# A decoder layer on one core: folded weight chunks begun before a group of seven, turns one step later, and a twelfth group with sums made ahead

## The chip, the core and the metric

The kernel runs on one core of a Trainium2 chip. The metric is device time of one execution in microseconds (us); the kernel before takes 2227.09 us, the median of 3 runs. A matmul here has a weight tile of 128x128 and streams 512 columns. TensorE is PE, VectorE DVE, ScalarE ACT, GpSimd POOL, and SyncE, which issues most transfers, SP.

## What is computed

A decoder layer for 256 tokens of width 2048 in float32: half a SwiGLU feed-forward, then retention and windowed attention side by side, a second half feed-forward, and a gated embedding, each with a layer norm behind it. The change touches the two feed-forwards:

```python
def swiglu(x, w_gu, w_down):
    g, u = jnp.split(x @ w_gu, 2, axis=-1)
    return (jax.nn.silu(g) * u) @ w_down
...
    h = layer_norm(alpha * h + 0.5 * swiglu(h, w_ffn1_gu[i], w_ffn1_down[i]), ln_g[i, 0], ln_b[i, 0])
...
    h = layer_norm(alpha * h + 0.5 * swiglu(h, w_ffn2_gu[i], w_ffn2_down[i]), ln_g[i, 2], ln_b[i, 2])
```

`w_gu` is 2048 x 11264, `w_down` 5632 x 2048.

## The kernel before

Every float32 factor is split in two parts, high and low, and a product is three matmuls: high by low, high by high, low by high (L431 to L433). The tokens' parts stay on chip, the weights stream through. A **chunk** is 512 KB of weights. SP loads it raw (L119), ACT casts it to the high part (L105), DVE subtracts the high part from the raw chunk for the low part (L106), PE uses both.

The work is a list of units (`plan`), each of them a pair of chunks or one chunk, written in the order in which PE will use them:

- **Single**: one chunk, 12 matmuls, one cast, one subtract. "P" is two Singles.
- **Folded**: one chunk whose low part DVE does not make. ACT multiplies the raw chunk by −1 into the place of the low part (here with the high part ahead of it in the order of `make`), POOL issues a transfer that adds the raw chunk to it (L170), and ACT casts the high part. "F" is a Single and a Folded, 24 matmuls.
- **Seven** ("S"): a pair of chunks as a product with seven instead of eight sub-products, 21 matmuls rather than 24, at the price of four sums (L226 to L229) and four subtracts on DVE and four casts on ACT.
- **Prepared** ("D"): a Seven whose sums were made earlier, in the mixer stages, by `sums_ahead` (L298 to L311), stored to DRAM, and are loaded back: one subtract for each of two raw tiles, four more loads.

A feed-forward's first product goes through 11 columns (j) of 512, each with 8 pairs p of chunks in the depth. Column 0 is eight P. Feed-forward 1 orders the others "FFSSFSSP": pairs 4 and 5 folded, Sevens 0 and 1, pair 6 folded, Sevens 2 and 3, pair 7. In feed-forward 2, `AHEAD` (L44) lists the columns with Prepared groups: odd columns 1 to 7 have two, even columns 2 to 6 one ("P?SSDSSP"), eleven in all; column 8 is "PFSSFSSP", 9 and 10 are as in feed-forward 1. The second product has four blocks of 512 output columns, done two at a time, so that a pair of chunks p (22 of them) serves two blocks; `FIRST_DOWN` (L51) orders the pairs of the first such block.

What sets the order ahead of PE is `fill` (L316). It runs each time that PE is done with a unit. It makes loaded units (casts, sums, subtracts) while less than 45 matmuls are ready, and loads further units of the plan while less than 90 are ready or loaded, as long as slots are free. All tiles live in a pool of 46 slots (`SLOTS`); `slots_for_weights` says how many the planner may use in a stage: 24 in feed-forward 1, 36 − j in feed-forward 2. A Folded's multiplication and transfer so begin in the place that the chunk has in the plan.

When a column is done, its result is activated and **turned** (`turned`, L984): cast into two 16-bit words on ACT, transposed by a transfer that SP issues (L189), joined on ACT. `later(DELAY, ...)` puts the transpose one step (one unit) after the words and the joining three steps behind it. The turned data is the left factor of the second product.

At the end of a block with Sevens, `seven_common` (from L546) combines four partial sums on ACT and DVE (`eve`, `evw`), which frees the banks that the next block writes.

Of the kernel before, what the change touches and what calls it, by code (L numbers as in the profile page):

```python
# [9 lines left out]
F32R = mybir.dt.float32r  # L10
# [40 lines left out]
FIRST_DOWN = "PPPPPPFFSFSPSFSPSFSSPS"  # L51
SECOND_DOWN = "PPPSPSPSFSPSFSSPSPPPPP"
LEAD = 4

# [8 lines left out]
def layer(ctx: ExitStack, tc: tile.TileContext, io):  # L63
# [24 lines left out]
    plan = []  # L88
# [51 lines left out]
    class Single:  # L140
# [7 lines left out]
        def load(self, **how):  # L148
            self.chunk = Chunk(self.key, **how)
# [1 line left out]
        def make(self):  # L151
            self.chunk.make()

    class Folded:

        loads, makes, keeps, time = 1, 2, 2, 12

        def __init__(self, key):  # L160
            self.key = key

        def load(self, **how):
            self.chunk = Chunk(self.key, **how)

        def make(self):
            c = self.chunk
            c.make_hi()
            act.mul(c.lo, c.raw, -1.0)
            pool.dma_start(c.lo, c.raw, accum_op=ALU.add)  # L170
            act.copy(c.hi, c.raw)

    class Turn:

# [141 lines left out]
    def fill(must=False):  # L316

        while True:
            queued = sum(u.time for u in ready)
            left = room["slots"] - room["used"]  # L320
            wanted = must and not ready or not room["quiet"] and queued < room["ahead"]
            if loaded and wanted and loaded[0].makes <= left:
                u = loaded.pop(0)
                u.make()
                room["used"] += u.keeps - u.loads
                ready.append(u)
                continue
            first = loaded[0] if loaded else plan[0] if plan else None
            queued += sum(u.time for u in loaded)
            if plan and queued < room["far"] and plan[0].loads + first.makes <= left:  # L330
                u = plan.pop(0)
                u.load()
                room["used"] += u.loads
                loaded.append(u)
                continue
            return

    def make_next():
# [4 lines left out]
        ready.append(u)  # L343

    def take(key):
        if not ready:
            fill(True)
        u = ready.pop(0)
        assert u.key == key, (u.key, key)
        return u  # L350
# [5 lines left out]
    def slots_for_weights(n, ahead=45, far=90):  # L356
        room.update(slots=n, ahead=ahead, far=far)
# [616 lines left out]
    def ffn(name, i, ht, norm, keep, residual, keepers, away):  # L974
# [33 lines left out]
        for j in range(KF // 4):  # L1008
            pg, pu = banks(f"{name}g{j}"), banks(f"{name}u{j}")
            units = gu_units(name, j)  # L1010
            n_of = {(0, 0): KD, (0, 1): KD, (1, 0): KD, (1, 1): KD}
            for kind, p in units:
                if kind in "SD":
                    for at in ((0, 0), (0, 1), (1, 0)):
                        n_of[at] -= 1
                    n_of[1, 1] -= 2
            sums = [[Sum((pg, pu)[n][t], n_of[t, n]) for n in range(2)] for t in range(2)]
            got = []

            if norm is not None and j == 0:  # L1020
                front, units = units[:FRONT_PAIRS], units[FRONT_PAIRS:]
                steps = [(gu_keys(name, 0)(n, p), 2 * p, n) for _, p in front for n in range(2)]
                norm.by_transfer = 3,
                norm.first(steps, rhs, sums, (
                    (3, (1, 0)), (5, "more"), (5, (1, 1)), (7, (0, 2)), (8, (1, 2)), (9, (0, 3)), (9, (1, 3)),
                    (10, ("move", 3)), (10, "go"),
                ))
                later(1, lambda: norm.join(3))
                slots_for_weights(24)

            def before(u, j=j, offset=KD // 2 - len(units)):
                u += offset
                if j == 0 and norm is None and u % 2 == 0:
                    first_chunk(u // 2)
                    if u == 6:
                        slots_for_weights(24)
                    if u == 2:
                        load_constants()
                if j == 0 and u == 7:
                    for g in sorted({p // 2 for p in SEVEN}):  # L1040
                        hi, lo = (slot([P, 8, P], F32R, f"{name}f{w}{g}") for w in "hl")
                        made[g] = seven_forms(keep[g], hi, lo)
                    if name == "f2":
                        g = AHEAD[1][0] // 2
                        made[g] = forms_of([ht[:, 4 * g : 4 * g + 4, :]], f"{name}f{g}")
                if name == "f2" and j and u == 0:
                    slots_for_weights(AHEAD_SLOTS - j)
                if j == KF // 4 - 1 and u in (4, 6):
                    convert(u // 2 - 2)

            block(f"{name}{j}", units, gu_keys(name, j), rhs, forms, sums, lambda *a: got.extend(seven_common(*a)), before)
            if got:
                g, v = got
                for x, ps in ((g, pg), (v, pu)):
                    for t in range(2):
# [158 lines left out]
    def mixers(ht, norm, residual, keepers, away):  # L1214
# [295 lines left out]

        made = {}
        forms = lambda p: made[p // 2](p % 2)
        lazy.append(sums_ahead(ahead[6:9], 2, 2))
        slots_for_weights(18)
        sig = []
        for j in range(4):
# [76 lines left out]

        lhs = lambda k: of_pairs(mix_t, k)
        slots_for_weights(16)
        lazy.append(sums_ahead(ahead[9:], 3, 2))

        def residual_added(blk, ps):
            for t in range(2):
# [344 lines left out]
```

## Time and profile before

| | us |
|---|---|
| median of 3 runs | 2227.09 (2226.49 to 2227.42) |
| the profiled execution | 2230.62 |
| its span in the profile | 2228.6 |
| PE busy in it | 2218.5 |
| DVE busy | 2004.0 |
| ACT busy | 1439.0 |
| POOL busy | 50.9 |

The span of the profile reaches from the first to the last instruction; the execution's own time is 2.0 us longer. Busy times are sums over the whole span. A row of a wait gives the waiting engine and line, what it waited for, and then the sum, the number and the longest of these waits. A row of a window gives the stretch, its length, busy time of each engine with its number of instructions, the granted clock of PE as a share, the busy share of the DMA engines, and GB/s.

### The profile page before, as it was taken

Reading aid. Unit: us, or ns where it says so; the run is one execution under the profiler, and the core shown is the slowest. Engines: PE = TensorE matmul, PEld = TensorE weight load, DVE = VectorE, ACT = ScalarE, POOL = GpSimd, SP = SyncE. Lnnn points to the kernel's source line nnn. Section 1 sums busy time; section 2 is a strip of 40 time slices with the busy share of each in tenths; the row PEclk is TensorE's granted clock in tenths of the full one; section 3 lists DMA queues with packets and bytes.
Section 4 is the critical chain, followed back from the end, with each engine's and each line's share of the span. In section 5 each row is a group of like instructions: output and inputs, shape, how many; then the busy total and the mean of one; then the engine's idle time right before and its main releaser. Section 6 shows DMA issues by size and latency. Waiting matters only on the chain.

```text
span 2228.6 us, 29103 instructions
## 1 busy us (share of the span) xinstructions
PE 2218.5 (100%) x10140; PEld 1838.9 (83%) x10140; DVE 2004.0 (90%) x2624; ACT 1439.0 (65%) x1677; POOL 50.9 (2%) x65
## 2 busy tenths in 40 slices
PE   9999999999999999999999999999999999999998
PEld 8888888888888888888788888888888888888887
DVE  6999999989998789789999888779999999999977
ACT  6777777777565545557865567466766677765653
POOL 0000000000000000000000000000000000000000
PEclk9999999999999999999999999999999999999999
DMA  9988998976686889757976568888999999666871
GB/s 321 250 264 252 249 263 241 269 227 217 228 305 234 298 283 338 203 179 232 291 233 226 184 203 321 316 302 266 301 301 295 300 248 276 209 233 221 309 283 68
DMA packets 302075, 570.51 MB, mean 256 GB/s; under 512 B 98652, under 2 KB 103388, under 8 KB 301928
## 3 DMA queue, kind: packets, MB, share of 16 engines
q1 hardware_dynamic: 291880, 536.71, 72.3%
q0 software_dynamic: 8064, 29.36, 7.0%
q10 hardware_dynamic: 1984, 2.58, 0.4%
q8 instruction: 79, 1.29, 0.2%
q14 instruction: 68, 0.56, 0.1%
HBM read 487.32 MB, written 31.46 MB: 233 GB/s over the span
## 4 chain that ended last, share of the span: by engine, by line
PE 93%; DMA 3%; DVE 2%; issue 1%; ACT 0%; SPq 0%; ACTq 0%; POOL 0%; DVEq 0%; POOLq 0%
PE rqk L382 3%; PE f2g L431 3%; PE f2g L433 3%; PE f2g L432 3%; PE f1g L431 2%; PE f1g L433 2%; PE f1g L432 2%; PE f2u L431 2%; PE f2u L433 2%; PE f2u L432 2%; PE f1u L433 2%; PE f1u L431 2%; PE f1u L432 2%; PE aqk L382 2%; PE f2e L431 1%; PE f1e L431 1%
## 5 line engine op out<-in xcount | busy, mean ns | idle before, releaser
L106 DVE TENSOR_TENSOR lf_gu<-rf_gu,hf_gu 128x1024 fp32r<-128x1024 f32 (+1 forms) x225 | 267.7, 1210 | 22.1 <-ACT hf_gu L105 21.1
L105 ACT CAST hf_gu<-rf_gu 128x1024 fp32r<-128x1024 f32 (+1 forms) x225 | 228.7, 1039 | 22.1 <-DMA rf_gu<-in_f_gu 21.5
L106 DVE TENSOR_TENSOR lw_in_f<-rw_in_f,hw_in_f 128x1024 fp32r<-128x1024 f32 x140 | 167.8, 1219 | 15.0 <-ACT hw_in_f L105 15.0
L106 DVE TENSOR_TENSOR lf_down<-rf_down,hf_down 128x1024 fp32r<-128x1024 f32 x130 | 155.7, 1220 | 12.9 <-ACT hf_down L105 11.1
L105 ACT CAST huf_gu<-uf_gu 128x1024 fp32r<-128x1024 f32 x76 | 80.1, 1053 | 125.4 <-DVE uf_gu L227 109.4
L105 ACT CAST hf_down<-rf_down 128x1024 fp32r<-128x1024 f32 x130 | 132.7, 1049 | 30.5 <-DMA rf_down<-in_f_down 21.3
L105 ACT CAST hw_in_f<-rw_in_f 128x1024 fp32r<-128x1024 f32 x140 | 140.4, 1049 | 2.3 <-PE gt L433 1.6
L105 ACT CAST hvf_gu<-vf_gu 128x1024 fp32r<-128x1024 f32 x76 | 80.1, 1054 | 32.4 <-DVE vf_gu L229 30.5
L106 DVE TENSOR_TENSOR luf_gu<-uf_gu,huf_gu 128x1024 fp32r<-128x1024 f32 x76 | 92.6, 1218 | 0.0
L106 DVE TENSOR_TENSOR lvf_gu<-vf_gu,hvf_gu 128x1024 fp32r<-128x1024 f32 x76 | 92.6, 1218 | 0.0
L431 PE MATMUL f1g<-hf_gu,xt 128*128 128x512 f32 x232 | 90.8, 391 | 0.0
L433 PE MATMUL f1g<-lf_gu,xt 128*128 128x512 f32 x232 | 90.5, 390 | 0.0
L432 PE MATMUL f1g<-hf_gu,xt 128*128 128x512 f32 x232 | 90.5, 390 | 0.0
L431 PE MATMUL f2g<-hf_gu,ht 128*128 128x512 f32 x211 | 82.2, 390 | 0.0
L433 PE MATMUL f2g<-lf_gu,ht 128*128 128x512 f32 x211 | 82.1, 389 | 0.0
L432 PE MATMUL f2g<-hf_gu,ht 128*128 128x512 f32 x211 | 82.1, 389 | 0.0
L433 PE MATMUL f1u<-lf_gu,xt 128*128 128x512 f32 x192 | 75.0, 391 | 1.2 <-DMA lf_gu<-rf_gu 1.2
L431 PE MATMUL f1u<-hf_gu,xt 128*128 128x512 f32 x192 | 74.7, 389 | 0.0
L432 PE MATMUL f1u<-hf_gu,xt 128*128 128x512 f32 x192 | 74.7, 389 | 0.0
L170 POOL DMA_DIRECT2D lf_gu<-rf_gu x42 | 36.4, 867 | 1641.2 <-DMA rf_gu<-in_f_gu 1017.6
L105 ACT CAST huf_down<-uf_down 128x1024 fp32r<-128x1024 f32 x32 | 33.7, 1054 | 60.7 <-DVE uf_down L227 58.7
L1057 ACT ACTIVATE eve<-eve 128x1024 f32<-128x1024 f32 x20 | 21.2, 1061 | 67.3 <-DVE eve L1056 67.3
(1512 smaller groups left out, 6978.3 us busy)
## 6 DMA issues: line engine op xcount, KB each, us to landing
rf_gu<-in_f_gu SPq DMA_DIRECT2D x361, 512.0 KB
rf_down<-in_f_down SPq DMA_DIRECT2D x176, 512.0 KB
rw_in_f<-in_w_in_f SPq DMA_DIRECT2D x148, 512.0 KB
lf_gu<-rf_gu POOLq DMA_DIRECT2D x42, 512.0 KB, 8.2
rw_rv<-in_w_rv SPq DMA_DIRECT2D x32, 512.0 KB
rw_ret<-in_w_ret SPq DMA_DIRECT2D x32, 512.0 KB
rw_mix<-in_w_mix SPq DMA_DIRECT2D x32, 512.0 KB
rw_pg<-in_w_pg SPq DMA_DIRECT2D x32, 512.0 KB
```

The lines of the kernel that those rows point to most:

```text
L105: act.copy(dst_hi, src)
L106: (lo_engine or dve).tensor_tensor(dst_lo, src, dst_hi, ALU.subtract)
L170: pool.dma_start(c.lo, c.raw, accum_op=ALU.add)
L382: pe.matmul(ps[f], hi[:, kk, f * P : (f + 1) * P], rhs(k), start=k == 0, stop=k == n_k - 1,)
L431: pe.matmul(o, al, bh, start=first, stop=False)
L432: pe.matmul(o, ah, bh, start=False, stop=False)
L433: pe.matmul(o, ah, bl, start=False, stop=self.left == 0)
L1057: act.activation(g, g, AF.Silu)
```

## The change

Folded is cut in two. A Folding, which takes no time on PE, loads the chunk, multiplies it and begins the accumulating transfer; the Folded that is left casts the high part at its old place and frees the Folding's two slots. `fold_at` puts the Folding into the plan 34 matmuls ahead of the Folded for first products and 12 for the second; if a Seven stands there or up to twelve units before, it goes back to just ahead of the nearest one. `AHEAD` gains pair 4 of column 8, so that column's order becomes "PFSSDSSP" and twelve groups have their sums made ahead, the second list of them with one group more. `DELAY` becomes 2. `FIRST_DOWN` gets one more F, and its two adjacent Sevens (17 and 18) are parted by pair 20. The first feed-forward's planner may use 30 slots.

```diff
+FOLD_AHEAD = 12, 34
-AHEAD = {1: (4, 5), 2: (4,), 3: (4, 5), 4: (4,), 5: (4, 5), 6: (4,), 7: (4, 5)}
+AHEAD = {1: (4, 5), 2: (4,), 3: (4, 5), 4: (4,), 5: (4, 5), 6: (4,), 7: (4, 5), 8: (4,)}
-DELAY = 1
+DELAY = 2
-FIRST_DOWN = "PPPPPPFFSFSPSFSPSFSSPS"
+FIRST_DOWN = "PPPPPFFSFSFSPSFSPSFSPS"
...
-    class Folded:
-        loads, makes, keeps, time = 1, 2, 2, 12
+    class Folding:
+        loads, makes, keeps, time = 1, 1, 2, 0
...
         def make(self):
             c = self.chunk
-            c.make_hi()
+            c.lo = slot(list(c.raw.shape), F32R, "l" + c.name)
             act.mul(c.lo, c.raw, -1.0)
             pool.dma_start(c.lo, c.raw, accum_op=ALU.add)
+
+    class Folded:
+        loads, makes, keeps, time = 0, 1, 2, 12
+        def __init__(self, begun):
+            self.key, self.begun = begun.key, begun
+        def load(self):
+            pass
+        def make(self):
+            c = self.chunk = self.begun.chunk
+            c.hi = slot(list(c.raw.shape), F32R, "h" + c.name)
             act.copy(c.hi, c.raw)
+            room["used"] -= self.begun.keeps
+
+    def fold_at(ahead, key):
+        begun = Folding(key)
+        at, time = len(plan), 0
+        while at > 0 and time < ahead:
+            at -= 1
+            time += plan[at].time
+        if ahead and any(isinstance(u, Seven) for u in plan[at - 12 : at + 1]):
+            while not isinstance(plan[at], Seven):
+                at -= 1
+        plan.insert(at, begun)
+        plan.append(Folded(begun))
...
             elif kind == "F":
-                plan.extend(of(keys(n, p)) for n, of in enumerate((Single, Folded)))
+                plan.append(Single(keys(0, p)))
+                fold_at(FOLD_AHEAD[keys(1, p)[0][-3:] == "_gu"], keys(1, p))
...
-                        slots_for_weights(24)
+                        slots_for_weights(30)
...
-        lazy.append(sums_ahead(ahead[3:6], 2, 2))
+        lazy.append(sums_ahead(ahead[3:7], 2, 2))
```

(The other two lists shift by one; `fill` and `take` leave units without time out of the ready list.)

ACT at the end of column 5 of feed-forward 1. In a name such as `hf1_gu_6_1_4`, h is a high part (l a low part, r raw, u and v sums), then stand the column, the chunk of the pair, and the pair; the last number counts tiles. Before:

```order
L105 CAST hvf1_gu_5_0_2_2123<-vf1_gu_5_0_2_2107 128x1024
L105 CAST hf1_gu_5_0_3_2147<-rf1_gu_5_0_3_2051 128x1024
L105 CAST bf1_gu_5_0_3_2151<-rf1_gu_5_1_3_2053 128x512
L105 CAST huf1_gu_5_0_3_2154<-uf1_gu_5_0_3_2141 128x1024
L105 CAST hvf1_gu_5_0_3_2158<-vf1_gu_5_0_3_2142 128x1024
L196 COPY f1a4_2164<-mf14_2055 128x2x4x128 x2
L105 CAST hf1_gu_5_0_7_2179<-rf1_gu_5_0_7_2083 128x1024
L105 CAST hf1_gu_5_1_7_2206<-rf1_gu_5_1_7_2127 128x1024
L105 CAST hf1_gu_6_0_4_2235<-rf1_gu_6_0_4_2162 128x1024
L169 ACTIVATE lf1_gu_6_1_4_2240<-rf1_gu_6_1_4_2183 128x1024
L171 CAST hf1_gu_6_1_4_2239<-rf1_gu_6_1_4_2183 128x1024
```

And of the change, where the multiplication is L170 and the cast L187:

```order
L107 CAST hvf1_gu_5_0_2_2127<-vf1_gu_5_0_2_2111 128x1024
L170 ACTIVATE lf1_gu_6_1_4_2145<-rf1_gu_6_1_4_2054 128x1024
L170 ACTIVATE lf1_gu_6_1_5_2148<-rf1_gu_6_1_5_2056 128x1024
L107 CAST hf1_gu_5_0_3_2157<-rf1_gu_5_0_3_2058 128x1024
L107 CAST bf1_gu_5_0_3_2161<-rf1_gu_5_1_3_2060 128x512
L107 CAST huf1_gu_5_0_3_2164<-uf1_gu_5_0_3_2151 128x1024
L107 CAST hvf1_gu_5_0_3_2168<-vf1_gu_5_0_3_2152 128x1024
L107 CAST hf1_gu_5_0_7_2186<-rf1_gu_5_0_7_2085 128x1024
L226 COPY f1a4_2190<-mf14_2087 128x2x4x128 x2
L107 CAST hf1_gu_5_1_7_2214<-rf1_gu_5_1_7_2131 128x1024
L107 CAST hf1_gu_6_0_4_2241<-rf1_gu_6_0_4_2172 128x1024
L187 CAST hf1_gu_6_1_4_2245<-rf1_gu_6_1_4_2054 128x1024
```

The multiplications of pairs 4 and 5 of column 6 went from behind pair 7 of column 5 to ahead of its fourth Seven (pair 3); the joining (COPY) moved one chunk back.

SP's loads for column 8 of feed-forward 2 (chunk 0 or 1, then the pair). Before:

```order
L119 DMA rf2_gu_8_0_6_16017<-in_f2_gu 128x2x512
L119 DMA rf2_gu_8_1_6_16031<-in_f2_gu 128x2x512
L119 DMA rf2_gu_8_0_2_16069<-in_f2_gu 128x2x512
L119 DMA rf2_gu_8_1_2_16071<-in_f2_gu 128x2x512
L119 DMA rf2_gu_8_0_3_16089<-in_f2_gu 128x2x512
L119 DMA rf2_gu_8_1_3_16091<-in_f2_gu 128x2x512
L189 DMA_TRANSPOSE mf27_16093<-wf27_16033 128x16x128
```

And of the change:

```order
L121 DMA rf2_gu_8_0_4_16044<-in_f2_gu 128x2x512
L287 DMA rf2_gu_8_0_4b_16046<-in_f2_gu 128x2x256
L291 DMA huf2_gu_8_0_4_16048<-hudf2_gu_8_0_4_12589 128x1024
L291 DMA luf2_gu_8_0_4_16050<-ludf2_gu_8_0_4_12590 128x1024
L291 DMA hvf2_gu_8_0_4_16052<-hvdf2_gu_8_0_4_12591 128x1024
L291 DMA lvf2_gu_8_0_4_16054<-lvdf2_gu_8_0_4_12592 128x1024
L121 DMA rf2_gu_8_0_2_16068<-in_f2_gu 128x2x512
L121 DMA rf2_gu_8_1_2_16070<-in_f2_gu 128x2x512
L121 DMA rf2_gu_9_1_4_16169<-in_f2_gu 128x2x512
L121 DMA rf2_gu_9_1_5_16171<-in_f2_gu 128x2x512
L121 DMA rf2_gu_8_0_3_16173<-in_f2_gu 128x2x512
L121 DMA rf2_gu_8_1_3_16175<-in_f2_gu 128x2x512
```

The Prepared group's six loads took the place of a folded pair, and two chunks of column 9 now stand ahead of the loads of the fourth Seven (pair 3).

SP's loads at the end of the first down block of feed-forward 1 (block, then the pair). Before:

```order
L119 DMA rf1_down_0_20_4717<-in_f1_down 128x1024
L119 DMA rf1_down_1_20_4777<-in_f1_down 128x1024
L119 DMA rf1_down_0_17_4779<-in_f1_down 128x1024
L119 DMA rf1_down_1_17_4781<-in_f1_down 128x1024
L119 DMA rf1_down_0_18_4803<-in_f1_down 128x1024
L119 DMA rf1_down_1_18_4805<-in_f1_down 128x1024
L119 DMA rf1_down_0_21_4911<-in_f1_down 128x1024
L119 DMA rf1_down_1_21_4938<-in_f1_down 128x1024
L119 DMA rf1_down_0_19_4965<-in_f1_down 128x1024
L119 DMA rf1_down_1_19_4967<-in_f1_down 128x1024
```

And of the change:

```order
L121 DMA rf1_down_1_20_4740<-in_f1_down 128x1024
L121 DMA rf1_down_0_17_4742<-in_f1_down 128x1024
L121 DMA rf1_down_1_17_4744<-in_f1_down 128x1024
L121 DMA rf1_down_0_20_4766<-in_f1_down 128x1024
L121 DMA rf1_down_0_18_4833<-in_f1_down 128x1024
L121 DMA rf1_down_1_18_4835<-in_f1_down 128x1024
L121 DMA rf1_down_0_21_4853<-in_f1_down 128x1024
L121 DMA rf1_down_1_21_4911<-in_f1_down 128x1024
L121 DMA rf1_down_0_19_4913<-in_f1_down 128x1024
L121 DMA rf1_down_1_19_4915<-in_f1_down 128x1024
```

Pair 20 moved between the Sevens 17 and 18, its second chunk, which is folded, ahead of 17.

More of the change, by code (lines that the diff above doesn't have):

```diff
@@ L152, in make, with load @@
             self.chunk.make()
-    class Folded:
-        loads, makes, keeps, time = 1, 2, 2, 12
+    class Folding:
+        loads, makes, keeps, time = 1, 1, 2, 0
         def __init__(self, key):
             self.key = key
-        def load(self, **how):
-            self.chunk = Chunk(self.key, **how)
+        def load(self):
+            self.chunk = Chunk(self.key)
         def make(self):
             c = self.chunk
-            c.make_hi()
+            c.lo = slot(list(c.raw.shape), F32R, "l" + c.name)
             act.mul(c.lo, c.raw, -1.0)
             pool.dma_start(c.lo, c.raw, accum_op=ALU.add)
-            act.copy(c.hi, c.raw)
+    class Folded:
+        loads, makes, keeps, time = 0, 1, 2, 12
+        def __init__(self, begun):
+            self.key, self.begun = begun.key, begun
+        def load(self):
+            pass
+        def make(self):
+            c = self.chunk = self.begun.chunk
+            c.hi = slot(list(c.raw.shape), F32R, "h" + c.name)
+            act.copy(c.hi, c.raw)
+            room["used"] -= self.begun.keeps
[10 more added lines that the diff above has]
+        plan.append(Folded(begun))
     class Turn:
@@ L322, in fill @@
             if loaded and wanted and loaded[0].makes <= left:
[L323 to L326, printed above, removed]
+                make_next()
                 continue
@@ L342, in make_next @@
         room["used"] += u.keeps - u.loads
-        ready.append(u)
+        if u.time:
+            ready.append(u)
     def take(key):
-        if not ready:
+        while not ready:
             fill(True)
@@ L1512, in mixers @@
         forms = lambda p: made[p // 2](p % 2)
-        lazy.append(sums_ahead(ahead[6:9], 2, 2))
+        lazy.append(sums_ahead(ahead[7:10], 2, 2))
         slots_for_weights(18)
@@ L1595, in mixers @@
         slots_for_weights(16)
-        lazy.append(sums_ahead(ahead[9:], 3, 2))
+        lazy.append(sums_ahead(ahead[10:], 3, 2))
         def residual_added(blk, ps):
```

## The prediction

> **What bounds the kernel now.** I read the page's busy line first, then the chain that ended last, then PE's waits, and only then the stages.
>
> ```profile
> PE 2218.5 (100%) x10140; PEld 1838.9 (83%) x10140; DVE 2004.0 (90%) x2624; ACT 1439.0 (65%) x1677; POOL 50.9 (2%) x65
> DVE  6999999989998789789999888779999999999977
> PEclk9999999999999999999999999999999999999999
> PE 93%; DMA 3%; DVE 2%; issue 1%; ACT 0%; SPq 0%; ACTq 0%; POOL 0%; DVEq 0%; POOLq 0%
> ```
>
> PE works in 2218.5 of 2228.6 us, at full granted clock throughout, and 93% of the chain is PE. DVE, at 90%, is close behind and owns 2% of the chain; DMA owns 3%. So there are two ways to save time: fewer matmuls, or the few places where PE waits. PE's list of waits names them:
>
> ```profile
> PE f1u L433 <- DMA lf_gu<-rf_gu: 1.2, 2, 0.9
> PE f1e L431 <- DVE evw L550: 0.6, 1, 0.6
> PE mr1a L433 <- DVE lw_ret L106: 0.5, 1, 0.5
> PE f2e L431 <- DVE evw L550: 0.5, 1, 0.5
> ```
>
> The change touches three of these four rows: the two waits for an accumulating transfer (first row), and the turn from the first to the second block of each down product (f1e, f2e). The third lies in the mixers, whose own order is not edited. Columns of the feed-forwards, cut at their first matmul, show what a column costs:
>
> ```profile
> core 0: us, PE busy (x) PEld busy (x) DVE busy (x) ACT busy (x) POOL busy (x), PEclk, DMA share, GB/s
> 50.10:92.10 42.00, 41.12 (x182) 33.73 (x181) 37.64 (x46) 30.53 (x34) 2.58 (x3) 1.00 0.97 270
> 92.10:132.90 40.80, 40.80 (x182) 33.78 (x181) 38.61 (x47) 29.53 (x33) 2.60 (x3) 1.00 0.82 237
> 214.50:255.90 41.40, 41.06 (x181) 33.67 (x180) 38.56 (x47) 31.54 (x35) 2.59 (x3) 1.00 0.96 251
> 378.30:419.30 41.00, 41.00 (x181) 33.71 (x180) 38.60 (x47) 30.82 (x34) 2.58 (x3) 1.00 0.92 254
> 460.10:574.40 114.30, 114.30 (x506) 94.64 (x505) 104.92 (x123) 80.55 (x85) 4.32 (x5) 1.00 0.69 222
> 874.60:900.00 25.40, 25.40 (x124) 21.45 (x123) 22.07 (x51) 11.96 (x15) 0.00 (x0) 1.00 0.80 269
> 900.00:923.20 23.20, 23.20 (x107) 19.30 (x106) 15.65 (x21) 16.08 (x21) 0.00 (x0) 1.00 0.96 285
> 1694.90:1735.10 40.20, 40.20 (x179) 33.26 (x179) 38.75 (x47) 27.34 (x31) 0.86 (x1) 1.00 0.93 304
> 1775.20:1816.00 40.80, 40.80 (x182) 33.78 (x181) 38.61 (x47) 29.49 (x33) 2.58 (x3) 1.00 0.90 258
> ```
>
> The rows are columns 1, 2, 5 and 9 of feed-forward 1, its first down block, two pieces of the retention stage, and columns 6 and 8 of feed-forward 2. A column of 180 matmuls takes 40.80 us undisturbed, that is 40.80/180 = 0.2267 us a matmul. Columns 1, 5 and 9 take 1.2, 0.6 and 0.2 us more, and in 1 and 5 the DMA share is 0.97 and 0.96.
>
> **The accumulating transfers.** A Folded chunk's low part is an ACT multiplication, then a transfer that POOL issues. The chain through column 1, and below it the one through column 5:
>
> ```profile
> 62.48 0.97 ACT lf_gu L169
> 63.45 0.28 issue
> 63.73 10.93 DMA lf_gu<-rf_gu
> ...
> 74.70 0.50 PE f1u L433
> 75.20 0.23 PE f1u L431
> ```
>
> ```profile
> 229.58 8.92 DMA lf_gu<-rf_gu
> ...
> 238.54 0.50 PE f1u L433
> ```
>
> ```profile
> lf_gu<-rf_gu POOLq DMA_DIRECT2D x42, 512.0 KB, 8.2
> ```
>
> From multiplication to use there were 74.70 − 62.48 = 12.2 us, and multiplication, issue and a landing of 10.93 took all of it. After the change the Folding that does this stands ahead of the fourth Seven of the column before: for pair 4 that is 21 matmuls of the Seven, 24 of the last pair and 12 of its own Single, so 57 × 0.2267 = 12.9 us sooner. Pair 5 moves by 24 more; pair 6 passes two Sevens and a Single, 54 matmuls or 12.2 us. The room doubles to about 24 us, more than twice the longest landing I found. The ACT order shows two multiplications ahead of the fourth Seven's casts: 2 × 0.97 = 1.9 us in front of them, on an engine that is busy 30.53 of 42.00 us. I cost that at nothing; without that cover it would be those 1.9 us a column. The gain is (42.00 + 41.40 + 41.00) − 3 × 40.80 = **−2.0 us**; its bounds are 0 and −2.0.
>
> The Trainium skill (DMA: Bandwidth & Descriptors, section "Anatomy of one DMA — SWDGE (gpsimd) path") fits a transfer issued by GpSimd as 2.0 us plus its bytes over 436e3 per us, an estimate of 3.2 us for 512 KB. By it no Folded could be late, this term would be 0 and the sum 2.0 higher. The row with 8.2 us contradicts it here: these transfers accumulate, and share queues that are busy 82 to 97%. I go by the row; the time that the rule gives is that of the second rival below, to whose chance it adds nothing.
>
> **Three matmuls fewer.** Column 8 of feed-forward 2 becomes one like column 6, with one group whose sums were made ahead: 40.20 instead of 40.80 by the windows, 3 × 0.2267 = 0.68 by the count. I take **−0.7**. The hidden price is DVE's, as column 6 shows:
>
> ```profile
> 1712.21 0.68 DVE L226 TENSOR_TENSOR uf_gu<-rf_gu,rf_gu 128x512 f32<-128x512 f32 x1
> 1724.90 1.22 DVE L106 TENSOR_TENSOR lvf_gu<-vf_gu,hvf_gu 128x1024 fp32r<-128x1024 f32 x1
> ```
>
> ```profile
> L433 PE MATMUL f26s<-lvf_gu,f2fh x2: 389/389/389, 1724.0 to 1726.7; 128*128 128x512 f32 x2
> ```
>
> ```profile
> 558.00 5.72 DMA rf_down<-in_f_down
> ```
>
> In column 6 (the first two fences: DVE's timeline, and PE's use of the tile) the fourth Seven's last subtract ends at 1724.90 + 1.22 = 1726.12 and PE needs it at 1726.7, with about 0.6 us left. In the changed column 8 the SP order puts this Seven's second load 59 matmuls (13.4 us) ahead of its use, behind two loads for column 9. DVE's eight operations on it are four sums and four subtracts, 4 × 0.68 + 3 × 1.22 + 0.68 = 7.1 us. From the load's issue 6.3 us remain for it to land, 8.1 where only the last tile counts, which PE needs 8 matmuls later. A plain load on the chain took 5.72 us (third fence), which is less; the longest accumulating transfer, 10.93, would be 10.93 − 8.1 = 2.8 too long. So the bounds are 0 and +2.8, once; I take 0, from the nearer row, that of a plain load.
>
> Making the sums costs four sums and two subtracts in the retention stage, 4 × 0.68 + 2 × 1.22 = 5.2 us of DVE, two casts on ACT and 3 MB of transfers. In the two retention windows DVE is idle for 3.3 and 7.5 us, and PE never is. I take 0. The bounds are 0 and +5.2. What would take the cover away is the 0.96 of the DMA share in the second window, where 3 MB at 285 GB/s are 10.5 us of transfers.
>
> **The turn of the down blocks.** The first block's end on DVE (first fence: its wait in that stage; second: its timeline; third: the chain):
>
> ```profile
> DVE uf_down L226 <- DMA rf_down<-in_f_down: 3.3, 1, 3.3
> ```
>
> ```profile
> 570.51 4.62 DVE L106 TENSOR_TENSOR lf_down<-rf_down,hf_down 128x1024 fp32r<-128x1024 f32 x4
> 575.05 0.68 DVE L550 TENSOR_TENSOR evw<-eve,f1d0s 128x512 f32<-128x512 f32 x1
> ```
>
> ```profile
> 575.13 0.61 DVE evw L550
> 575.79 0.50 PE f1e L431
> 576.29 0.23 PE f1e L432
> ```
>
> DVE stands 3.3 us for the load of the last Seven (pair 19), does its eight operations and four subtracts for the next block, and is late for evw, which frees the bank that PE needs. In the new order a pair of 24 matmuls stands between pairs 17 and 18, and the loads of 19 wait for 17's slots: by the waits in the order they now go out 97 matmuls before the block's end and no longer 79, 18 × 0.2267 = 4.1 us sooner. That covers the 3.3 us. One subtract (1.22 us) goes too, since one more chunk is folded; its multiplication goes to ACT, which is busy 80.55 of 114.30 us there. So both waits go: 0.6 + 0.5 = **−1.1**. The first matmul after each wait also took 0.50 rather than 0.23; if that is part of the wait, the gain is 1.1 + 2 × 0.27 = 1.6. I take 1.1, as no row shows such a turn without a wait. Bounds 0 and −1.6.
>
> **Turns a step later.** The transposes on SP stand behind casts on ACT:
>
> ```profile
> SPq L189 <- ACT hf_gu L105: 24.0, 4, 10.8
> ```
>
> Such a wait holds every load queued behind it. One step later the words are there when SP reaches them. No wait of PE goes back to SP, so I take 0, and as bounds −0.5 and +0.5, the size of the smaller waits in PE's list: the turned data is next used in the down product, and only the last column's has little time.
>
> **The sum.** The profiled execution took 2230.62 us, 2.0 above its span and 3.5 above the median of 2227.09. −2.0 − 0.7 − 1.1 = −3.8 gives 2226.8 for a profiled execution. I assume that timed runs have the same waits and predict 2227.09 − 3.8 = **2223.3**.
>
> **The rivals.**
>
> *The turn restarts for free*: all 1.6 go, the sum is −4.3, 2222.8. For it: both first matmuls after a wait have 0.50, also behind the accumulates (74.70, 238.54). Against it: DVE must be done in time at both turns. 20%.
>
> *The accumulates do not gain*: the waits are made by a saturated DMA (0.97) and move to the loads that the earlier transfers displace, or they belong to the profiled execution alone, which is 3.5 us longer. Then −0.7 − 1.1 = −1.8, 2225.3. For it: all the excess columns have shares of 0.92 to 0.97, and the number of transfers is the same. Against it: column 2, at 0.82, lost nothing, and 12.9 us is more than any landing. 22%. That the change does nothing beyond the three matmuls would be 2226.4; I count it here.
>
> *Begun chunks crowd out the fourth Seven*, the slower side: a begun chunk holds raw and product, two slots, for 12.9 us more; three of them are six. Feed-forward 1 gets six more slots, feed-forward 2 none, and the fourth Seven's loads come behind the Foldings. Its last tile has 0.6 us to spare in column 6. If it came late in every column with a Folding before it (10 of feed-forward 1, 7 of feed-forward 2), each by as much as an accumulate did, 1.2/2 = 0.6 us, that would be 17 × 0.6 = 10.2 us: 2233.5. It decides against the change from 3.8/17 = 0.22 us a column on. For it: the orders of column 8. Against it: in feed-forward 1 DVE, not the loads, sets when that Seven is done, and its loads still lead by over 85 matmuls. 8%.
>
> **How the numbers follow.** The forecast has 50%, the rivals 20, 22 and 8. About 0.2% (4.45 us) is what a measurement of this kernel can tell from no change: faster means below 2222.64, slower above 2231.54. Of the forecast a fifth falls below 2222.64 (0.10), of the first rival half (0.10): faster 0.20. The last rival is slower: 0.08. The rest, 0.72, is within 0.2%. The range runs from 2221.8 (both full gains, the turn's 1.6 and 0.5 of the transposes, and 0.5 of spread) to 2227.3 (2225.3 with 2 us of the column's and the sums' bounds); it leaves out the last rival and the thin ends.
>
> **What would show it.** Right: all columns of feed-forward 1 but the first at 40.8 us, column 8 of feed-forward 2 near 40.2; the rows of PE's waits on lf_gu and evw gone, and DVE's wait of 3.3 us; one more accumulating transfer in all. Wrong: PE waiting for luf_gu or lvf_gu in column 8 or in the columns with a Folding (crowding); PE still waiting on lf_gu, with landings of 10 us or more in spite of the earlier start (saturated DMA); PE waiting for lw_in_f between 875 and 925 us (sums made ahead); evw still late (turn).

## The result, and the profile after

The changed kernel takes 2244.34 us, the median of 5 runs (2241.44 to 2249.93), against 2227.42 us before (2226.49 to 2228.39): a ratio of 1.0079, with a 95% interval of 1.0064 to 1.0094. It is 17 us slower. The forecast was 2223.3, and 2227.3 at the most. The five runs differ by 8.5 us from each other, those of before by 1.9.

The profiled execution took 2241.44 us, the fastest of the five. Its busy line and PE's list of waits (engine and line, what it waited for, sum, times, longest; line numbers are those of the changed kernel, 2 to 30 higher):

```profile
PE 2221.0 (99%) x10137; PEld 1839.2 (82%) x10137; DVE 2006.0 (90%) x2629; ACT 1441.8 (64%) x1680; POOL 51.9 (2%) x66
```

```profile
PE f2u L459 <- ACT hf_gu L107: 6.6, 1, 6.6
PE f28s L461 <- DVE lf_gu L108: 2.2, 2, 1.6
...
PE f28s L461 <- DVE luf_gu L108: 0.8, 1, 0.8
PE mr1a L461 <- DVE lw_ret L108: 0.5, 1, 0.5
```

Three matmuls are gone, and so are all three rows that the change was to touch, the waits for accumulating transfers and for evw. In their place stands one wait of 6.6 us for a cast in feed-forward 2, and after it some for DVE. The windows show columns 1, 5 and 9 of feed-forward 1, then columns 4, 7 and 8 of feed-forward 2, cut as before:

```profile
core 0: us, PE busy (x) PEld busy (x) DVE busy (x) ACT busy (x) POOL busy (x), PEclk, DMA share, GB/s
50.10:90.90 40.80, 40.80 (x182) 33.80 (x181) 39.21 (x48) 32.50 (x37) 2.59 (x3) 1.00 0.96 292
213.30:254.10 40.80, 40.80 (x182) 33.80 (x181) 38.60 (x47) 30.65 (x34) 2.60 (x3) 1.00 0.95 258
376.50:417.30 40.80, 40.80 (x182) 33.80 (x181) 38.69 (x47) 31.01 (x34) 2.59 (x3) 1.00 0.93 253
1611.90:1652.80 40.90, 40.64 (x178) 33.04 (x177) 40.07 (x49) 28.28 (x31) 0.86 (x1) 1.00 0.92 294
1733.10:1782.90 49.80, 43.18 (x178) 34.72 (x177) 33.00 (x40) 25.52 (x29) 0.86 (x1) 0.90 1.04 253
1782.90:1827.50 44.60, 41.50 (x179) 32.93 (x177) 43.51 (x55) 30.25 (x33) 1.72 (x2) 1.00 0.85 264
```

The three columns of feed-forward 1 stand at 40.80, as forecast. A column of 177 matmuls takes 177 × 0.2267 = 40.1 us undisturbed; column 7 takes 9.7 us more, column 8 4.5 more and column 4 0.8 more, together 15.0. The profiled execution is 2241.44 − 2230.62 = 10.8 us longer than the one of before, so everything else gained 4.2: 2.0 in columns 1, 5 and 9, 0.7 for three matmuls, 1.5 at the two turns of the down blocks. In this execution the forecast's sum came; 15 us that it did not have came on top. The medians differ by 16.9 us, 6.1 more than the profiled executions: the profiled one of before lies 3.2 above its median, that of the change 2.9 below. Of the other executions there is no trace.

What happened in column 7 stands in the DMA view from 1755 to 1775 us (40 slices of half a microsecond: busy tenths of the DMA engines, and what they moved):

```profile
DMA  9993898999999003998999979966897992589999
GB/s 296 297 190 87 183 264 23 21 24 31 45 105 6 8 9 14 151 36 39 51 62 109 30 49 37 104 44 51 65 88 96 77 108 46 105 268 381 369 373 369
```

For some 14 us the engines are reported busy nearly throughout and move 6 to 150 GB/s, where about 370 GB/s are moved just behind. Two transfers are in flight there, by the rows of their tiles in this part of the program: the transpose of column 6, which SP issued at 1750.2 us, and the transfer of column 8's Folding, which POOL issued at 1753.3 us.

```profile
L219 SPq DMA_TRANSPOSE mf<-wf x2: 6862/7208/7554, 1750.2 to 1803.2; - x2
```

```profile
L171 POOL DMA_DIRECT2D lf_gu<-rf_gu x1: 862/862/862, 1753.3 to 1753.3; - x1
...
DMA to landing us min/median/max: 21.5/21.5/21.5
```

The transfer landed after 21.5 us; the longest before was 10.9. In the packet records, the transpose's 2048 packets of 256 bytes ran from 1755.2 to 1772.7 us, 17.4 us, and 118 of the 128 packets of POOL's transfer fell among them. In the kernel before no transpose of a feed-forward took over 4.9 us, and none had more than 15 such packets in it. The loads that SP issued behind the transpose land late. The chain of waits shows the one that PE missed, a load of 18.16 us:

```profile
1757.88 18.16 DMA rf_gu<-in_f_gu
```

Why the two meet is in the order of the changed kernel. By my count in it, the turns of columns 2 to 6 of feed-forward 2 and the multiplication of the nearest Folding are released within 5 to 7 matmuls of each other (1.1 to 1.6 us); before the change these were 42 to 87 matmuls apart. The Folding moved forward and the transpose back, towards each other. The executions differ from the order in size, not in kind: ACT began the multiplication 3.2, 6.4, 1.5, 3.9 and 1.5 us behind SP's start of the transpose in columns 2 to 6; before the change 13.6 to 20.2 us lay between the two.

### The profile page after: what moved, and what is told of

Its sections match the earlier page's. It is cut to its first block, busy times and chain, and to the rows that moved or that the text cites. A ratio compares the mean times of both kernels' runs of the same rounds, so it can differ in the third digit from the quotient of the medians.

```text
span 2239.7 us, 29171 instructions
## 1 busy us (share of the span) xinstructions
PE 2221.0 (99%) x10137; PEld 1839.2 (82%) x10137; DVE 2006.0 (90%) x2629; ACT 1441.8 (64%) x1680; POOL 51.9 (2%) x66
## 4 chain that ended last, share of the span: by engine, by line
PE 92%; DMA 3%; DVE 3%; issue 1%; ACT 1%; SPq 0%; ACTq 0%; DVEq 0%
PE f1g L461 3%; PE f1g L459 3%; PE f1g L460 3%; PE rqk L410 3%; DMA rf_gu<-in_f_gu 2%; PE f1u L461 2%; PE f1u L459 2%; PE f1u L460 2%; PE f2g L459 2%; PE f2g L460 2%; PE f2g L461 2%; PE f2u L461 2%; PE f2u L459 2%; PE f2u L460 2%; PE aqk L410 2%; PE f2e L461 1%
## 5 line engine op out<-in xcount | busy, mean ns | idle before, releaser
L459 PE MATMUL f2u<-hf_gu,ht 128*128 128x512 f32 x160 | 63.6, 398 | 6.6 <-ACT hf_gu L107 6.6
```

The source lines that it names most:

```text
L459: pe.matmul(o, al, bh, start=first, stop=False)
```

## The experiments

All are compared with the kernel before on the same chip, whose median there was 2229.2 to 2229.3. The changed kernel itself was not run again beside them. Theory 1: a transpose and a transfer of POOL's that run at the same time hold each other up, with all that is queued behind. Theory 2, the rival, is the prediction's crowding: begun chunks hold slots, and the loads of column 8 are late.

**One turn moved back.**

```diff
-            later(DELAY, turn.move)
-            later(DELAY + 3, joined)
+            wait = 1 if name == "f2" and j == 6 else DELAY
+            later(wait, turn.move)
+            later(wait + 3, joined)
```

> One turn alone goes back: the change with column 6 of feed-forward 2 turned one step after its step as before the change, all other turns two steps. Theory 1 (a transpose and an accumulating transfer whose packets meet on the DMA engines hold each other up, and everything queued behind them): the multiplication of column 8's Folding then stands 45 matmuls behind the transpose of column 6 and no longer 6 ahead of it, the stall of column 8 (6.7 us at its first load, some 14 us with what follows) is gone; 2226 to 2232, since turns 2 to 5 keep their distance of 5 to 7 matmuls and may still meet. Theory 2 (crowding: begun chunks and the twelfth prepared group push the loads of column 8 back, whatever the turn does): 2240 or more, column 8 still waits over 5 us.

Measured: 2229.05 us (2226.41 to 2234.87), a ratio of 1.0002 (0.9994 to 1.0011). One transpose, one step earlier, as theory 1 expected, takes the stall of column 8's loads away, with every slot and load of the Foldings as it was. In its profiled execution (2234.22 us) the transpose of column 4, still close to a Folding, met one instead: 11.3 us long, 73 of POOL's packets in it. Columns 5, 6 and 7 there:

```profile
1651.52:1692.16 40.64, 40.28 (x179) 33.04 (x177) 30.17 (x36) 24.63 (x28) 0.86 (x1) 1.00 1.02 265
1692.16:1737.83 45.67, 41.85 (x178) 32.86 (x179) 44.63 (x55) 30.09 (x33) 0.86 (x1) 1.00 0.93 308
1737.82:1777.94 40.12, 40.12 (x178) 33.22 (x177) 37.15 (x46) 27.16 (x30) 0.86 (x1) 1.00 0.92 303
```

Column 7 is back at 40.12. In column 5, where the meeting falls, DVE works only 30.17 us; column 6 pays 5.5 us while DVE catches up, busy 44.63 of 45.67.

**All turns moved back.**

```diff
-DELAY = 2
+DELAY = 1
```

> The change with all turns one step later only, as before the change. Theory 1 (transpose and accumulating transfer meet): distances of turns 2, 3, 5, 6 in feed-forward 2 become 14 to 74 matmuls, only turn 4 stays within 3; 2223 to 2227. Theory 2 (crowding): no change against the changed kernel, 2240 or more.

Measured: 2227.03 us, a ratio of 0.9991 (0.9982 to 0.9999), 2.3 us faster than before, by an interval that hardly leaves out no difference. No transpose of feed-forward 2 exceeded 3.5 us, and none had a packet of POOL's in it, not even that of column 4, which the order puts within 3 matmuls of a Folding: in the execution the multiplication began 3.8 us behind SP's start of that transpose. Theory 2 expected 2240.

**Foldings of feed-forward 2 moved back.**

```diff
-FOLD_AHEAD = 12, 34
+FOLD_AHEAD = {"f1_gu": 34, "f2_gu": 0}
...
-                fold_at(FOLD_AHEAD[keys(1, p)[0][-3:] == "_gu"], keys(1, p))
+                fold_at(FOLD_AHEAD.get(keys(1, p)[0], 12), keys(1, p))
```

> The change with the Foldings of the first products of feed-forward 2 at their old place in the plan (those of feed-forward 1 and of the down products stay early), turns two steps later. Theory 1 (meeting) : turns 2 to 6 are 66 to 74 matmuls from the nearest accumulating transfer; 2222.5 to 2225, which is the forecast's sum. Theory 2 (crowding by begun chunks): the same 2222.5 to 2225, but also by crowding of the prepared group alone: 2230 or more.

Measured: 2226.71 us, a ratio of 0.9990 (0.9981 to 0.9998); the profiled execution took 2226.67. Columns 6, 7 and 8 of feed-forward 2:

```profile
1692.31:1732.43 40.12, 40.12 (x178) 33.23 (x177) 39.29 (x48) 27.85 (x31) 0.86 (x1) 1.00 0.85 265
1732.43:1772.55 40.12, 40.12 (x178) 33.23 (x177) 36.45 (x44) 27.12 (x30) 0.86 (x1) 1.00 1.04 342
1772.55:1812.67 40.12, 40.12 (x178) 33.23 (x177) 38.21 (x47) 28.78 (x32) 1.72 (x2) 1.00 0.92 282
```

All three are undisturbed, column 7 at the same DMA share of 1.04 as in the changed kernel: it is not the load on the DMA engines as such. The turns stand two steps later here as well, so a later turn costs nothing by itself. Moving either of the two away from the other is enough. The expected 2222.5 to 2225 was too low, by what the section on why the prediction was wrong says of the sum.

**Without the twelfth group.** (The lists of `sums_ahead` are those of before as well.)

```diff
-AHEAD = {..., 7: (4, 5), 8: (4,)}
+AHEAD = {..., 7: (4, 5)}
```

> The change without the twelfth prepared group: column 8 of feed-forward 2 as before, eleven groups, lists as before. Theory 1 (meeting): turns 2 to 6 still stand 5 to 7 matmuls from an accumulating transfer; 2230 to 2248. Theory 2 (crowding by the prepared group's loads in column 8): 2224 to 2227.

Measured: 2250.10 us, a ratio of 1.0090 (1.0077 to 1.0104). That is above both expectations, on theory 1's side. The prepared group's loads are not the cause; without them it is worse than the changed kernel's 2244.34, and in the profiled execution two turns meet a transfer with 98 and 128 packets, where in the changed kernel's it was 44 and 118. Columns 5, 6, 7 and 8:

```profile
1650.68:1694.54 43.86, 40.86 (x178) 32.89 (x176) 30.16 (x36) 24.62 (x28) 0.86 (x1) 1.00 1.03 249
1694.54:1740.21 45.67, 41.84 (x177) 32.88 (x178) 44.63 (x55) 30.11 (x33) 0.86 (x1) 1.00 0.93 304
1740.21:1794.38 54.17, 42.31 (x178) 33.83 (x176) 30.94 (x38) 24.84 (x28) 0.86 (x1) 0.91 1.01 189
1794.38:1839.37 44.99, 42.21 (x181) 33.50 (x181) 43.84 (x54) 32.42 (x35) 2.60 (x3) 1.00 0.96 291
```

The transpose of column 4 took 14.7 us, that of column 6 24.2 us, with all 128 of POOL's packets among its own, at 189 GB/s over the whole of column 7.

**The collision by itself, and its twin.** In the kernel before, at each turn of the feed-forwards:

```diff
-            sync.dma_start_transpose(
+            (act if self.name[0] == "f" else sync).dma_start_transpose(
...
+            if self.name[0] == "f":
+                for h in range(2):
+                    pool.dma_start(self.src[:, h], self.words[:, 1].rearrange("p a n -> p (a n)").bitcast(F32), accum_op=ALU.add)
-DELAY = 1
+DELAY = 0
```

and in the twin with `self.moved[:, 1].rearrange("p a b n -> p (a b n)")` as the source.

> The kernel before with an added transfer at each of the 22 turns of the feed-forwards: two accumulating transfers of 256 KB add words of the turned data to a tile that is no longer needed, and start when the words are there; the transposes are issued by ACT right behind the words, no step later, so that both run at the same time. The added sums are used by nothing. Theory 1 (a transpose and an accumulating transfer that run together hold each other up): transposes take 7 us and more where their packets overlap, instead of 2.5 to 5; the time rises by 20 to 150 us against the twin with the same transfers behind the transposes. Theory 2 (they don't matter to each other, the stall of the changed kernel comes from crowded slots): within 3 us of the twin.

> The twin: the same 44 transfers, with the turned data as their source, so that each starts only when the transpose has landed; the transposes are issued by ACT as well. The added sums are used by nothing. Theory 1: transposes of 2.5 to 5 us, the time within 10 us of the kernel before (11.5 MB more to move). Theory 2: the same as the kernel in which they meet, within 3 us.

Measured: 2351.38 us for the pair that meets (ratio 1.0541, 1.0525 to 1.0557) and 2373.07 for the twin (1.0655, 1.0639 to 1.0672). The transposes went only in part as theory 1 has it: a median of 7.7 us and up to 24.2 against 3.7 and up to 12.9 in the twin, where none of POOL's packets fell among theirs. But five transposes of the pair that meets took under 5 us with 19 to 80 of POOL's packets among their own, and five of the twin took 9.6 to 12.9 us without one. In both kernels ACT issues the transposes, so that SP's loads run beside them on another queue. By the packet records SP's queue moved 0.8 to 2.9 MB during those five transposes of the twin, and at most 0.5 MB during each of the other 17, which took 2.6 to 4.8 us. So a transpose can be long beside a queue other than POOL's. The total time did not follow theory 1: the twin is the slower one, and both are far from before, which neither theory expected. The waits of PE say why, first of the pair that meets, then of the twin:

```profile
PE f1u L436 <- DMA lf_gu<-rf_gu: 54.6, 9, 13.5
```

```profile
PE f1u L436 <- DMA lf_gu<-rf_gu: 78.2, 10, 16.9
PE f2u L436 <- DMA lf_gu<-rf_gu: 33.3, 3, 16.3
```

POOL issues in order. The added transfers wait there for the words, in the twin even for the transpose, and the Folded chunks' own transfers stand behind them. The control brought a wait of its own and tells nothing about the time.

**Plain transfers in place of accumulating ones.**

```diff
-            pool.dma_start(c.lo, c.raw, accum_op=ALU.add)
+            pool.dma_start(c.lo, c.raw.bitcast(F32R))
```

> The changed kernel with plain transfers in place of the accumulating ones, same queue, place, size and tiles; the addition is left out, so that the low parts of folded chunks are the raw chunks. Theory 1a (it takes the accumulation): transposes of 2.5 to 5 us beside these transfers too, the stall of column 8 is gone, 2222 to 2227. Theory 1b (any transfer of POOL's queue does it): 2236 or more.

Measured: 2236.72 us, a ratio of 1.0037 (1.0024 to 1.0049). Theory 1a falls: the transposes of columns 4 and 6 still took 10.8 and 10.4 us, with 95 and 126 plain packets among theirs. It takes a transfer of POOL's queue beside the transpose, but no addition. They cost less here, 9.7 us over the 2227 of the versions without meetings, against 17 with the addition.

**Turns three steps later.**

```diff
-DELAY = 2
+DELAY = 3
```

> The changed kernel with turns three steps later and no longer two. Theory 1 (meeting): multiplications of feed-forward 2 then stand 21 to 32 matmuls (4.8 to 7.3 us) ahead of the transposes, about the length of an accumulating transfer, so most have landed; 2224 to 2232. A theory by which a later turn costs by itself: 2244 or more.

Measured: 2238.45 us, a ratio of 1.0044 (1.0031 to 1.0056), outside what either theory expected. The transposes of columns 5 and 6 took 12.1 and 6.7 us, with 120 and 123 of POOL's packets among theirs, and columns 6 to 9 lost 4.7, 1.7, 4.2 and 3.0 us. The 21 to 32 matmuls of the order were not reached in the execution: ACT began the multiplications only 0.4 us (column 5) and 2.1 us (column 6) ahead of SP's start of the transpose, and POOL's transfers, which landed 15.8 and 11.2 us after their issue, were still in flight. So it is not only who comes first.

**Without the transfers.**

```diff
-            pool.dma_start(c.lo, c.raw, accum_op=ALU.add)
+            if self.key[0] != "f2_gu":
+                pool.dma_start(c.lo, c.raw, accum_op=ALU.add)
```

> The changed kernel without the transfers of the Foldings in the first products of feed-forward 2: their loads, multiplications, slots and places in the plan stay, only POOL's transfer is left out (their low parts are then the negated raw chunks). Theory 1 (those transfers meet the transposes): 2221 to 2227, transposes of 2.5 to 5 us. Theory 2 (begun chunks hold slots, push loads back or stand in ACT's way): 2240 or more.

Measured: 2226.62 us, a ratio of 0.9989 (0.9981 to 0.9998). Slots, loads, multiplications and the order of every engine but POOL are those of the changed kernel, and the loss is gone. This settles it against theory 2. Columns 7 and 8:

```profile
1731.73:1771.85 40.12, 40.12 (x178) 33.22 (x177) 34.77 (x42) 26.69 (x29) 0.00 (x0) 1.00 0.95 313
1771.86:1812.77 40.91, 40.71 (x179) 33.07 (x178) 39.94 (x50) 29.21 (x32) 0.00 (x0) 1.00 0.82 266
```

The 0.8 us in column 8 is all that crowding may have cost in this execution.

**Parts alone.** The early Foldings and 30 slots of feed-forward 1, nothing else. (The diff is against the change. `AHEAD` and the lists are those of before, and every other Folding stands directly ahead of its Folded.)

```diff
-FIRST_DOWN = "PPPPPFFSFSFSPSFSPSFSPS"
+FIRST_DOWN = "PPPPPPFFSFSPSFSPSFSSPS"
-FOLD_AHEAD = 12, 34
+FOLD_AHEAD = {"f1_gu": 34}
-DELAY = 2
+DELAY = 1
```

> One part alone: the kernel before with the early Foldings of feed-forward 1 and its 30 slots, nothing else of the change. If the waits for accumulating transfers are in timed runs as in the profiled one: 1 to 2 us faster than before, and columns 1, 5 and 9 at 40.8 us in the profile. If they belong to the profiled execution, or come back as waits for loads: within 0.5 us of before, or those columns stay above 41.

Measured: 2228.29 us, a ratio of 0.9996 (0.9987 to 1.0005): 1.0 us, and its interval holds both no gain and 2 us. The profiled execution shows columns 1, 5 and 9 at 40.80. It also lacks both waits for evw, though the down blocks have their old order here and no Folding of feed-forward 2 is early.

The turns alone, two steps later in the kernel before (the diff is against that):

```diff
-DELAY = 1
+DELAY = 2
```

> One part alone: the kernel before with turns two steps later. Theory 1 (meeting): turns 2 to 6 of feed-forward 2 keep 66 matmuls and more from any accumulating transfer, the last three 5 to 23; 2226 to 2233. If a later turn costs by itself: 2240 or more.

Measured: 2233.03 us, a ratio of 1.0023 (1.0014 to 1.0032), the upper end of what theory 1 gave, but not for its reason: the last three turns of feed-forward 2 met no more than 16 packets. The profiled execution shows a meeting in feed-forward 1 instead, which the expectation had not looked at: the transpose of column 9 took 7.8 us, with 70 of POOL's packets, and PE waited for the chunk:

```profile
PE f1u L433 <- DMA lf_gu<-rf_gu: 2.5, 1, 2.5
```

Columns 1 and 5 of feed-forward 1 show something else here. Their Folded chunks begin at the old place, as in the kernel before, and yet the columns are undisturbed:

```profile
49.80:90.60 40.80, 40.80 (x181) 33.78 (x180) 37.62 (x46) 30.43 (x34) 2.59 (x3) 1.00 0.93 254
213.00:253.80 40.80, 40.80 (x181) 33.78 (x180) 38.60 (x47) 30.60 (x34) 2.60 (x3) 1.00 0.96 257
```

**Both undone** (the edits of the second and the third experiment together).

> The change with both parts undone that bring the two together: Foldings of feed-forward 2's first products at their old place, turns one step later; the early Foldings of feed-forward 1, the twelfth group and the new order of the down block stay. Theory 1: no meeting, the forecast's sum: 3 to 4.5 us faster than before. If the forecast's terms are not in timed runs: within 1 us of before.

Measured: 2226.97 us, a ratio of 0.9991 (0.9982 to 1.0000). At 2.3 us faster it lies between the two expectations; against either part undone alone nothing more is to be had.

The meetings of the profiled executions in one table, from the packet records. "f2 6" is column 6 of feed-forward 2; "loss" is the time of columns over 40.1 or 40.8 us, in columns with over 0.5. The first two medians were measured side by side, the others beside a median of before of 2229.2 to 2229.3:

| | transposes over 5 us (POOL's packets in them) | loss by column | median us |
|---|---|---|---|
| before | none | f1: 1.2, 0.6 | 2227.4 |
| the change | f2 2: 7.0 (44); f2 6: 17.4 (118) | f2 4: 0.8; 7: 9.7; 8: 4.5 | 2244.3 |
| turn 6 back | f1 1: 5.1 (0); f2 4: 11.3 (73) | f2 5: 0.5; 6: 5.5; 9: 2.2 | 2229.1 |
| all turns back | none | f2 6: 0.6 | 2227.0 |
| f2 Foldings back | none | none | 2226.7 |
| no twelfth group | f2 4: 14.7 (98); 6: 24.2 (128) | f2 5: 3.7; 6: 5.5; 7: 14.0; 8: 4.2 | 2250.1 |
| plain transfers | f2 4: 10.8 (95); 6: 10.4 (126) | f2 6: 5.1; 7: 1.1; 8: 5.4 | 2236.7 |
| turns 3 later | f2 5: 12.1 (120); 6: 6.7 (123) | f2 6: 4.7; 7: 1.7; 8: 4.2; 9: 3.0 | 2238.5 |
| no f2 transfers | none | f2 8: 0.8 | 2226.6 |
| f1 Foldings alone | none | none | 2228.3 |
| 2 later, alone | f1 9: 7.8 (70) | f1 10: 4.5 | 2233.0 |
| both undone | none | f2 9: 1.0 | 2227.0 |

On SP's queue every transpose of the feed-forwards with 44 or more of POOL's packets in it took 6.7 us or more, and none with fewer took over 5.1. Each profiled execution with a meeting of 60 packets or more lost 4 us or more. Which turns meet differs between executions of nearly the same order, and a few microseconds decide it: in the changed kernel the multiplication began 1.5 us behind the transpose in columns 4 and 6 alike, and the one had 16 of POOL's packets in it, the other 118. The spread of the timed runs fits this. From the lowest to the highest it is 8.4 to 10.3 us in the changed kernel and four of the five variants with a meeting (3.9 with plain transfers), and 2.3 to 3.5 us in the five without; the kernel before, run more often there, has 4.2 to 5.9.

## Why the prediction was wrong

**The step that failed** is "Turns a step later", where the prediction took 0 with bounds of ±0.5, and with it the part on the accumulating transfers, which weighed a Folding's start only against its use. Each was priced alone. The transpose moved back on SP and the Folding's transfer forward on POOL, and nothing asked whether they now fall together. The prediction priced a wait of SP on ACT and called it off the path; the price was a transpose of 17.4 us and the loads behind it, 15.0 us in three columns of the profiled execution. The order showed it: it puts the two within 5 to 7 matmuls in five turns. I had read ACT's order in feed-forward 1 only, where that distance is 15 and more by the order, and SP's in column 8 without its transposes.

**The rivals.** The slower rival, crowding, named the right column and the wrong cause: without the transfers, with all slots still held, the time is 2226.62. Its sign, PE waiting for luf_gu in column 8, did appear (0.8 us), but behind the stall, while DVE caught up. The 2.8 us bound for column 8's fourth Seven was not needed either; the 0.8 us that column 8 lost without the transfers is the most that it was there. The second rival named a DMA share of 0.92 to 0.97 as a sign of lost time; columns 1, 5 and 9 of the changed kernel have 0.93 to 0.96 and lost nothing. The sums made ahead cost nothing that the profile shows: PE has the same wait of 0.5 us in the mixers (mr1a) as before and none of that size beside it.

**The terms of the sum held in the profiled executions.** Columns 1, 5 and 9 went to 40.80 (−2.0, as forecast); a column of 177 matmuls takes 40.12 (−0.7); the waits at the turns of the down blocks went, and with them the longer first matmul (−1.5, close to the 1.6 of the first rival). But of two terms the reason that I gave is not shown. With the old order of the down blocks, the early Foldings of feed-forward 1 alone took both waits for evw away too. With every Folded at its old place, later turns alone left columns 1, 5 and 9 at 40.80 too. Both kinds of wait may sit at the edge of a margin that many changes move, or come and go from one execution to the next; a second profile of the kernel before would tell. The forecast for a profiled execution was 2226.8; three of the versions without meetings took 2226.67 to 2226.78, the fourth 2227.62. So good a hit is in part luck, as long as the causes of two of its three terms are open.

**In timed runs less of it came.** Those versions are 2.3 to 2.7 us faster than before, not 3.8. Their intervals (0.9981 to 1.0000 as ratios, or 0 to 4.2 us) hold both, so it stays open whether part of the waits belongs to the profiled execution alone, as the second rival had it.

The rule of the Trainium skill (DMA: Bandwidth & Descriptors, section "Anatomy of one DMA — SWDGE (gpsimd) path") on the length of a GpSimd transfer, 3.2 us for 512 KB as an estimate, is not met by the accumulating transfers. The row of all 41 in the changed kernel, and below it the row with plain transfers in their place, whose shortest come near the rule:

```profile
DMA to landing us min/median/max: 4.5/7.7/21.5
DMA to landing us min/median/max: 2.9/5.3/14.2
```

## What to carry to other kernels

When two edits move transfers of different queues, look up in the order what each new place stands beside, not only what it stands ahead of. How far apart is far enough, the executions say and not the order. Eleven profiled executions have the transposes on SP's queue and all of POOL's transfers, with 242 turns in all. In each of the ten meetings of 44 packets or more, ACT began the nearest multiplication between 2.1 us before and 3.2 us behind SP's start of the transpose; 20 more turns lie in that span and had 29 packets at the most. Outside it no turn had more than 16. Of an engine at 90% beside the bound, expect a stall to be paid twice: once when it stands, and again while it catches up.

## What the runs showed of the hardware

**A transpose beside another queue's transfers.** On SP's queue the 2048 packets of 256 bytes of a turn pass in 2.4 to 5.1 us when few or none of POOL's packets are among them. With a transfer of POOL's among them both crawl; in column 6 of the changed kernel single packets, with medians of 18 and 327 ns, took up to 1.9 and 3.8 us. Issued by ACT, a transpose took 9.6 to 12.9 us beside 0.8 to 2.9 MB of SP's loads as well, so POOL's queue is not the only one that does it. The Trainium skill (DMA: Bandwidth & Descriptors, section "Rules for kernel authors") says that a transpose next to ordinary transfers needs nothing. It says so where it warns of corrupted data, and not of time; in time the runs show a price. Why the engines do this no run here shows.

**A transpose on SP's queue holds SP.** SP's instruction alone took 3.9 us (median) before, and 6.9 in the changed kernel:

```profile
L219 SPq DMA_TRANSPOSE mf<-wf x22: 1323/6896/9692, 58.8 to 1917.7; - x22
```

I expected the later turn to make SP's part shorter. With two steps and nothing else the median is 4.9 us, longer than before. But three versions with the old turns and early Foldings have 4.7 to 5.0 us as well, so it is not shown that the later turn lengthens it.

**The clock.** When PE resumed after the wait of 6.6 us, its granted clock was halved for another 5.8 us:

```profile
1777.10:1782.90 5.80, 5.64 (x12) 3.96 (x13) 3.59 (x4) 5.80 (x8) 0.00 (x0) 0.50 1.05 387
```

12 matmuls took 5.8 us rather than 12 × 0.2267 = 2.7, so the wait cost 3.1 us more than itself. The wait of 2.5 us in the kernel with only later turns did it too, for a shorter time:

```profile
440.60:443.30 2.70, 0.16 (x2) 0.03 (x1) 2.60 (x4) 0.45 (x1) 0.00 (x0) 1.00 0.94 272
443.30:446.00 2.70, 2.70 (x9) 2.19 (x10) 2.67 (x5) 2.23 (x3) 0.00 (x0) 0.74 0.88 350
446.00:450.00 4.00, 4.00 (x14) 3.16 (x14) 3.65 (x5) 4.00 (x5) 0.00 (x0) 0.75 0.57 188
```

The 0.74 and 0.75 are means over stretches at full and at half clock: from 445.0 to 447.6 us the granted clock is 0.50. The column lost 4.5 us to that wait of 2.5. The Trainium skill (TensorE: Matmul & The Clock Gate, section "Part 1: The HAM clock gate (the "warmup" mystery)") has PE fall to half its clock after an idle window of about 3.4 us. The half clock agrees; an idle time of 2.5 us was enough here. The waits of up to 1.6 us in column 8 of the changed kernel left the clock at 1.00.
